# The 32x32 triangular blocks of a gated delta rule: 31 substitution steps on GpSimd in place of 15 steps and a merge on TensorE

## The chip, the cores and the metric

The kernel runs on one core of a Trainium2 chip, in one launch. The metric is the device time of a run in microseconds, and a version's time is the median over its runs. The core has a matrix engine (TensorE, PE in the profile), three engines for elementwise work (VectorE: DVE, ScalarE: ACT, GpSimd: POOL) and 16 DMA engines. DMAs are issued here mostly from the queue of SyncE (SP), some from POOL and ACT. Each engine takes its instructions in order and waits on semaphores for the others.

## The reference

One residual block works on 512 frames of width 1024. A projection feeds two token mixers, a gated delta rule with 8 heads and a convolution branch. Gates merge them, and a SwiGLU channel mixer follows. The change lies in the delta rule, whose chunks hold C frames (64 in the reference):

```python
gc = jnp.cumsum(g, axis=-1)
decay = jnp.exp(jnp.where(tril, gc[..., :, None] - gc[..., None, :], -jnp.inf))
kk = jnp.einsum("bnhid,bnhjd->bnhij", k, k)
m_low = jnp.where(strict, beta[..., :, None] * kk * decay, 0.0)
t_mat = m_low + jnp.eye(CHUNK, dtype=jnp.float32)
rhs = jnp.concatenate([v * beta[..., None], k * (beta * jnp.exp(gc))[..., None]], axis=-1)
sol = lax.linalg.triangular_solve(t_mat, rhs, left_side=True, lower=True, unit_diagonal=True)
...
def step(S, xs_c):
    v_new = u_c - jnp.einsum("bhcd,bhde->bhce", w_c, S)
    o_c = jnp.einsum("bhcd,bhde->bhce", qd_c, S) + jnp.einsum("bhij,bhje->bhie", a_c, v_new)
    S = S * el_c[..., None, None] + jnp.einsum("bhcd,bhce->bhde", kd_c, v_new)
```

So each head needs the inverse of unit triangular matrices, and then a recurrence over chunks that uses them. The output is the whole block's, with a final RMSNorm.

## The kernel before, in words

The kernel takes chunks of 128 frames, four to a head (`NT = 4`), so four 128x128 unit triangular matrices are inverted for each of the 8 heads. The inverse is built from small blocks upward.

The first phase, up to some 475 us, is a row of projections: 32 units for the heads (k, q, v and z of each), 12 for the convolution branch and 16 for the gates. A unit (`proj`) has 8 K steps of three matmuls each (`split3` on L118, a weight in a high and a low part). Its weight is loaded into `raw` by SP (L105), split into `whi` by ACT (L108) and `wlo` by DVE (L109), each in three buffers. The generator `step` walks through the K steps and counts them in `count`. A head owns 32 counts, and behind each head stand 12 or 8 counts of other units (`OTHERS`).

Three pieces of a head hang on this count:

- `front(h)` makes the matrix. It transposes and squares k, multiplies k with itself (L418), scales and masks it into `Un` (L421 on ACT, L422 on POOL) and copies the four diagonal 32x32 blocks into `cp` (L428). Behind the first head, all that `front` puts on POOL is queued behind the last substitution step of the head before (`issue_after(last[0].ins)`).
- The substitution, also in `front`, inverts the diagonal blocks. Coefficients go to DRAM (`sc`, L437) and come back broadcast over the partitions (`U`, L440), both on SP's queue. Then come the steps on POOL, each a multiply into `ytm` (L454) and an add into `y` (L456). Before the change the blocks are 16x16 and the steps 15; the masks `mh1` and `mh2` put the two 16x16 halves of each 32x32 block side by side.
- `chain(h)` takes `y` and is started when the count reaches `START + 32 h` plus the `OTHERS` of the heads before. It first merges pairs of 16x16 blocks to 32x32 (L481 to L498, with matmuls on L490 and L496), then 32 to 64 (L514, L522) and 64 to 128 (L534, L539). Then it runs the recurrence over four chunks (L552 to L578). Each `yield n` lets n counts pass. At its end a power on POOL (L586) gives the norm's factor, which ACT uses in `scaled` (L592) once 32 counts have passed.

Several tiles that the chain reads (`kT`, `qT`, `Un`, `Vp`, `at`, `kd`, `y`) have three buffers, so head h + 3 needs the chain of head h to be done with them.

The order on each engine is set by a planner that puts the instructions in order by their place in the program and by when it holds their inputs to be ready; `behind` and `issue_after` add edges that fix an order on one engine. From count 335 on, weight loads also start work for the later phases (`fill`): DRAM to DRAM copies and accumulating DMAs for sums of FFN weights (`feed_one`, L189 on SP and L193 on POOL), and sums of the down projection's weights (`half_load`, L163, and `dsums_add`, L169, L170, on POOL). The accumulating DMAs and the additions on POOL are queued behind `last[0]`, the last substitution step so far. Before the change the half loads of the first phase take a buffer of `U`.

The phases behind the first one multiply the two mixers' outputs, norm, and run the FFN. They don't touch the substitution.

Of the kernel before, what the change touches and what calls it, by code (L numbers as in the profile page):

```python
# [6 lines left out]
F32 = mybir.dt.float32  # L7
# [16 lines left out]
PAD3 = 368  # L24
START = 84
# [6 lines left out]
def block_kernel(ctx, tc, a):  # L32
# [17 lines left out]
    cst = base.tile([P, 7 * P + 18], F32, name="cst")  # L50
    ident, tri, suf, mid, ones, neg = (cst[:, i * P:(i + 1) * P] for i in range(6))

    mc = cst[:, 6 * P:7 * P]

    mh1, mh2, idc = cst[:, 7 * P:7 * P + 1], cst[:, 7 * P + 1:7 * P + 2], cst[:, 7 * P + 2:]
# [295 lines left out]
    Ye = gp.tile([P, NT, P], F32, name="Ye")  # L351
    for t in (X, Y, Q1, Q2, Xd, Yd, Yl, Ye):
        G.memset(t, 0.0)
# [45 lines left out]
    def front(h, kT, DT):  # L399
# [25 lines left out]
        cc = gp.tile([P, NT, 16], F32, name="cc")  # L425
# [3 lines left out]
        if h:  # L429
            G.tensor_scalar(out=cc, in0=cp[:, :, 0:16], scalar1=mh1, scalar2=None, op0=ALU.mult)  # L430
            G.tensor_scalar(out=cp[:, :, 0:16], in0=cp[:, :, 16:32], scalar1=mh2, scalar2=None, op0=ALU.mult)
            c_ = G.tensor_tensor(out=cc, in0=cc, in1=cp[:, :, 0:16], op=ALU.add)
# [4 lines left out]
        nc.sync.dma_start(sc.rearrange("b k n c -> (b k) n c"), cc)  # L437
        U = gp.tile([P, 16, NT, 16], F32, name="U", bufs=2)
        for b in range(8):
            nc.sync.dma_start(U[16 * b:16 * b + 16].rearrange("p k n c -> p (k n c)"),  # L440
                              sc[b].rearrange("k n c -> (k n c)").partition_broadcast(16))

        Ud = gp.tile([P, NT, P], F32, name="Ud", bufs=3)
        with tc.issue_after(c_.ins) if h else nullcontext():
            G.tensor_tensor(out=Ud, in0=Un, in1=mc.rearrange("p (a t) -> p a t", a=1).broadcast_to([P, NT, P]),
                            op=ALU.mult)


        y = gp.tile([P, NT, 16], F32, name="y", bufs=3)
        S.copy(out=y, in_=idc.rearrange("p (a c) -> p a c", a=1).broadcast_to([P, NT, 16]))  # L450
        for k in range(15):
            w = 15 - k
            tm = gp.tile([P, NT, 16], F32, name="ytm")
            G.tensor_tensor(out=tm[:, :, 0:w], in0=U[:, k, :, k + 1:],  # L454
                            in1=y[:, :, k:k + 1].broadcast_to([P, NT, w]), op=ALU.mult)
            last[0] = G.tensor_tensor(out=y[:, :, k + 1:], in0=y[:, :, k + 1:], in1=tm[:, :, 0:w], op=ALU.add)  # L456
        return ss, kd, b2, Un, Ud, y
# [839 lines left out]
```

## Time and profile before

| | us |
|---|---|
| median of 3 runs | 963.17 |
| lowest and highest of the runs | 961.48 and 963.8 |
| span of the profiled execution, first to last instruction | 961.9 |
| mean granted TensorE clock in it | 0.998 |

The profiled execution has no time of its own beside its span. The span lies within the runs shown, 1.3 us below their median.

A row of the profile names the line of the kernel, the engine and the operation, then the tile that is written and those that are read, the shape, and the count. After the bar it gives the busy time in us and the mean of one instruction in ns, then the idle time of the engine ahead of them and what ended it. A row of the timeline begins with the start and the duration in us; PE's matmuls overlap, so two of them can be busy at once.

### The profile page before, as it was taken

The page shows a single profiled execution, that of the slowest core. Times are in us where ns is not written, and L with a number is a line of the kernel's source. Part 1 is how long each engine was busy: PE and PEld are TensorE (multiplying, and loading weights), DVE is VectorE, ACT ScalarE, POOL GpSimd, SP SyncE. Part 2 cuts the span into 40 slices and gives each one's busy share as a digit, 9 for nine tenths or more (in the row PEclk, how much of TensorE's full clock was granted, in tenths as well). Part 3 has the DMA queues.
Part 4 walks back from the last instruction along what each step waited for, and adds up shares of the span by engine and source line. Part 5 has one row for each costly group of instructions (what it writes and reads, how often), then busy time and mean ns, then how long its engine had stood idle before and what let it go on. Part 6 is the DMA issues. An engine that isn't in the chain of part 4 may idle for free.

```text
span 961.9 us, 14869 instructions
## 1 busy us (share of the span) xinstructions
PE 941.8 (98%) x5199; PEld 793.8 (83%) x5199; DVE 731.8 (76%) x1118; ACT 529.4 (55%) x1095; POOL 357.4 (37%) x565
## 2 busy tenths in 40 slices
PE   6999999999999999999999999999999999999996
PEld 5687888888887887888887888888889999988885
DVE  4898888988888888888477763676525887889886
ACT  6588865867856775544547232423324545556554
POOL 0323645243463327534345342245451111134034
PEclk9999999999999999999999999999999999999999
DMA  9243423133231426988897985499899556578653
GB/s 310 94 143 101 123 66 92 59 116 102 66 103 55 129 82 176 279 253 248 257 297 221 288 277 175 174 272 281 294 252 224 191 184 193 174 221 268 212 192 134
DMA packets 78298, 177.39 MB, mean 184 GB/s; under 512 B 10208, under 2 KB 19328, under 8 KB 77200
## 3 DMA queue, kind: packets, MB, share of 16 engines
q1 hardware_dynamic: 66816, 144.88, 45.4%
q0 software_dynamic: 10256, 28.89, 13.3%
q10 hardware_dynamic: 1152, 2.69, 0.7%
q8 instruction: 41, 0.67, 0.3%
q14 instruction: 33, 0.27, 0.1%
HBM read 156.22 MB, written 45.37 MB: 210 GB/s over the span
## 4 chain that ended last, share of the span: by engine, by line
PE 90%; DVE 4%; ACT 2%; POOL 2%; issue 1%; DMA 1%; SPq 0%; POOLq 0%; ACTq 0%; DVEq 0%
PE mm L118 59%; PE w L118 20%; PE g L385 1%; PE st L564 1%; PE g L418 1%; PE st L558 1%; DVE wlo L109 1%; PE b L490 1%; PE st L563 1%; PE b L496 1%; DMA gsl<-sgd 1%; POOL ss L879 1%; PE b L514 1%; PE st L552 1%; PE g L467 1%
## 5 line engine op out<-in xcount | busy, mean ns | idle before, releaser
L108 ACT ACTIVATE whi<-raw 128x1024 fp32r<-128x1024 f32 (+1 forms) x191 | 196.4, 1030 | 246.8 <-PE mm L118 151.1
L109 DVE TENSOR_TENSOR wlo<-raw,whi 128x1024 fp32r<-128x1024 f32 (+1 forms) x191 | 242.3, 1270 | 95.9 <-ACT whi L108 95.3
L118 PE MATMUL mm<-hh,whi 128*128 128x512 f32 (+1 forms) x688 | 269.9, 393 | 0.5 <-ACT whi L108 0.3
L118 PE MATMUL mm<-hl,whi 128*128 128x512 f32 (+1 forms) x688 | 264.0, 384 | 2.3 <-POOL hl L300 1.6
L118 PE MATMUL mm<-hh,wlo 128*128 128x512 f32 (+1 forms) x688 | 263.9, 384 | 0.1
L620 DVE SCALAR_TENSOR_TENSOR cps<-c,c31w,cps 128x512 f32<-128x512 f32 x240 | 180.2, 751 | 4.3
L118 PEld LDWEIGHTS mm<-hl,whi 128*128 128x128 f32 x688 | 129.9, 189 | 24.7 <-POOL hl L300 2.9
L118 PEld LDWEIGHTS mm<-hh,wlo 128*128 128x128 f32 x688 | 129.6, 188 | 23.8 <-DVE wlo L109 0.6
L118 PEld LDWEIGHTS mm<-hh,whi 128*128 128x128 f32 x688 | 129.8, 189 | 22.7 <-ACT whi L108 0.8
L949 POOL TENSOR_TENSOR fm<-fm 128x256 f32<-128x256 f32 x33 | 29.8, 904 | 113.3 <-DVE s L949 90.1
L372 DVE SCALAR_TENSOR_TENSOR acc<-mm,c4w,acc 128x511 f32<-128x511 f32 (+2 forms) x72 | 53.0, 738 | 1.9 <-ACT acc L369 1.9
L118 PE MATMUL mm<-yh,whi 128*128 128x512 f32 x128 | 50.7, 396 | 0.0
L118 PE MATMUL mm<-yl,whi 128*128 128x512 f32 x128 | 50.0, 391 | 0.6 <-DVE yl L808 0.6
L454 POOL TENSOR_TENSOR ytm<-U,y 128x60 f32<-128x60 f32 (+14 forms) x120 | 31.8, 265 | 48.6 <-DMA U<-sc 30.9
L118 PE MATMUL mm<-yh,wlo 128*128 128x512 f32 x128 | 49.8, 389 | 0.0
L118 PE MATMUL w<-hh,wlo 128*128 128x256 f32 x168 | 47.7, 284 | 0.3 <-DVE wlo L109 0.3
L118 PE MATMUL w<-hh,whi 128*128 128x256 f32 x168 | 47.6, 284 | 0.0
L118 PE MATMUL w<-hl,whi 128*128 128x256 f32 x168 | 47.5, 283 | 0.0
L118 PE MATMUL w<-wlo,fh 128*128 128x512 f32 (+1 forms) x115 | 44.3, 385 | 0.2 <-DVE wlo L109 0.2
L118 PE MATMUL w<-whi,fl 128*128 128x512 f32 (+1 forms) x115 | 44.2, 384 | 0.0
L118 PE MATMUL w<-whi,fh 128*128 128x512 f32 (+1 forms) x115 | 44.2, 384 | 0.0
L456 POOL TENSOR_TENSOR y<-y,ytm 128x60 f32<-128x60 f32 (+14 forms) x120 | 39.0, 325 | 9.4
(324 smaller groups left out, 1904.0 us busy)
## 6 DMA issues: line engine op xcount, KB each, us to landing
raw<-in_win_dram SPq DMA_DIRECT2D x61, 512.0 KB, 3.5
raw<-in_wgu_dram SPq DMA_DIRECT2D x32, 512.0 KB, 3.5
s<-in_wgu_dram SPq DMA_DIRECT2D x48, 256.0 KB, 6.2
raw<-s SPq DMA_DIRECT2D x48, 256.0 KB, 3.8
raw<-wsum SPq DMA_DIRECT2D x44, 256.0 KB, 4.0
raw<-in_wdn_dram SPq DMA_DIRECT2D x33, 256.0 KB, 3.3
s<-in_wgu_dram POOLq DMA_DIRECT2D x24, 256.0 KB, 6.9
s<-s POOLq DMA_DIRECT2D x24, 256.0 KB, 7.0
```

Source lines behind the costliest of these rows:

```text
L108: marked(S.activation(hi, raw, AF.Copy), "unit")
L109: marked(V.tensor_tensor(out=lo, in0=raw, in1=hi.bitcast(F32), op=ALU.subtract), "unit")
L118: marked(PE.matmul(ps, l, r, start=first and i == 0, stop=last and i == 2))
L372: marked(V.scalar_tensor_tensor(out=acc[:, s:], in0=ps[:, :T - s], scalar=c4w[:, j, k:k + 1], in1=acc[:, s:], op0=ALU.mult, op1=ALU.add))
L385: PE.transpose(ps[:, n, :], src[:, n, :], ident)
L418: PE.matmul(ps[:, n, :], kT[:, n, :], kT[:, n, :], start=True, stop=True)
L454: G.tensor_tensor(out=tm[:, :, 0:w], in0=U[:, k, :, k + 1:], in1=y[:, :, k:k + 1].broadcast_to([P, NT, w]), op=ALU.mult)
L456: last[0] = G.tensor_tensor(out=y[:, :, k + 1:], in0=y[:, :, k + 1:], in1=tm[:, :, 0:w], op=ALU.add)
L467: PE.matmul(ps[:, n, :], kT[:, n, :], qT[:, n, :], start=True, stop=True)
L490: PE.matmul(ps[:, n, 0:16], Ud[:, n, :], xc[:, n, 0:16], start=True, stop=True)
L620: V.scalar_tensor_tensor(out=acc, in0=c[:, k:k + T], scalar=c31w[:, i, k:k + 1], in1=acc, op0=ALU.mult, op1=ALU.add)
L949: return eng.tensor_tensor(out=out, in0=in0, in1=in1, op=op)
```

## The change

The substitution works on the four 32x32 diagonal blocks of a matrix in 31 steps, so `y` leaves POOL as the inverse of 32x32 blocks. The merge of 16x16 blocks goes, and with it `Ud`, `Ye`, `Q0`, the masks and the constants for them. The coefficients go to DRAM in eight stores (rows 0 to 15 of each block whole, rows 16 to 31 with their second half only) and come back in four broadcast loads of 32 partitions. `U` grows from 4 KB to 12 KB per partition and has one buffer where it had two. The half loads of the first phase get a tile of their own with one buffer. The chain of head 0 starts 8 counts later and that of head 1 by 4 counts; the others keep their count. The first `yield`s of the chain (2 and 2) go with the merge. The padding is resized.

```diff
-PAD3 = 368
-START = 84
+PAD3 = 482
+START = (92, 88, 84, 84, 84, 84, 84, 84)
...
     def half_load():
         k, cs = halves.pop(0)
-        if len(gps_) == 1:
-            r = gps_[0].tile([P, 16, NT, 16], F32, name="U", bufs=2)
-            r = r.rearrange("p k n c -> p (k n c)").rearrange("p (i c) -> p i c", i=4)
-        else:
-            r = gps_[1].tile([P, 4, 256], F32, name="wsh", bufs=1)
+        r = gps_[-1].tile([P, 4, 256], F32, name="wsh", bufs=1)
...
         for b in range(4):
             b32 = slice(32 * b, 32 * b + 32)
             (G.tensor_copy if h else S.copy)(out=cp[b32], in_=Un[b32, :, b32])
-        if h:
-            G.tensor_scalar(out=cc, in0=cp[:, :, 0:16], scalar1=mh1, scalar2=None, op0=ALU.mult)
-            G.tensor_scalar(out=cp[:, :, 0:16], in0=cp[:, :, 16:32], scalar1=mh2, scalar2=None, op0=ALU.mult)
-            c_ = G.tensor_tensor(out=cc, in0=cc, in1=cp[:, :, 0:16], op=ALU.add)
-        else:
-            S.activation(cc, cp[:, :, 0:16], AF.Copy, scale=mh1)
-            V.scalar_tensor_tensor(out=cc, in0=cp[:, :, 16:32], scalar=mh2, in1=cc, op0=ALU.mult, op1=ALU.add)
-        sc = dram.tile([8, 16, NT, 16], F32, name="sc")
-        nc.sync.dma_start(sc.rearrange("b k n c -> (b k) n c"), cc)
-        U = gp.tile([P, 16, NT, 16], F32, name="U", bufs=2)
-        for b in range(8):
-            nc.sync.dma_start(U[16 * b:16 * b + 16].rearrange("p k n c -> p (k n c)"),
-                              sc[b].rearrange("k n c -> (k n c)").partition_broadcast(16))
-
-        Ud = gp.tile([P, NT, P], F32, name="Ud", bufs=3)
-        with tc.issue_after(c_.ins) if h else nullcontext():
-            G.tensor_tensor(out=Ud, in0=Un, in1=mc.rearrange("p (a t) -> p a t", a=1).broadcast_to([P, NT, P]),
-                            op=ALU.mult)
-        y = gp.tile([P, NT, 16], F32, name="y", bufs=3)
-        S.copy(out=y, in_=idc.rearrange("p (a c) -> p a c", a=1).broadcast_to([P, NT, 16]))
-        for k in range(15):
-            w = 15 - k
-            tm = gp.tile([P, NT, 16], F32, name="ytm")
-            G.tensor_tensor(out=tm[:, :, 0:w], in0=U[:, k, :, k + 1:],
+        sc = dram.tile([4, 3072], F32, name="sc")
+        U = gp.tile([P, 3072], F32, name="U")
+        for b in range(4):
+            nc.sync.dma_start(sc[b, 0:2048].rearrange("(k n c) -> k n c", k=16, n=NT), cp[32 * b:32 * b + 16])
+            nc.sync.dma_start(sc[b, 2048:].rearrange("(k n c) -> k n c", k=16, n=NT),
+                              cp[32 * b + 16:32 * b + 32, :, 16:])
+        for b in range(4):
+            nc.sync.dma_start(U[32 * b:32 * b + 32], sc[b].partition_broadcast(32))
+        U1 = U[:, 0:2048].rearrange("p (k n c) -> p k n c", k=16, n=NT)
+        U2 = U[:, 2048:].rearrange("p (k n c) -> p k n c", k=16, n=NT)
+        y = gp.tile([P, NT, 32], F32, name="y", bufs=3)
+        S.copy(out=y, in_=idc.rearrange("p (a c) -> p a c", a=1).broadcast_to([P, NT, 32]))
+        for k in range(31):
+            w = 31 - k
+            u = U1[:, k, :, k + 1:] if k < 16 else U2[:, k - 16, :, k - 15:]
+            tm = gp.tile([P, NT, 32], F32, name="ytm")
+            G.tensor_tensor(out=tm[:, :, 0:w], in0=u,
                             in1=y[:, :, k:k + 1].broadcast_to([P, NT, w]), op=ALU.mult)
             last[0] = G.tensor_tensor(out=y[:, :, k + 1:], in0=y[:, :, k + 1:], in1=tm[:, :, 0:w], op=ALU.add)
...
-    def chain(h, kT, qT, ss, kd, b2, Un, Ud, Vp, at, yq, zs):
+    def chain(h, kT, qT, ss, kd, b2, Un, Vp, at, y, zs):
         sq = junk[:, 0:P]
-        y = gp.tile([P, NT, 32], F32, name="yb")
         xc = gp.tile([P, NT, 32], F32, name="xc")
-        flat = lambda t: t.rearrange("p n c -> p (n c)")
-        S.activation(y[:, :, 0:16], yq, AF.Copy, scale=mh1)
-        S.activation(y[:, :, 16:32], yq, AF.Copy, scale=mh2)
-        V.transpose(out=flat(xc), in_=flat(y))
-        for b in range(4):
-            b32 = slice(32 * b, 32 * b + 32)
-            S.copy(out=Ye[b32, :, b32], in_=y[b32])
-        yield 2
-        ps = psb.tile([P, 4, P], F32, name="b")
-        for n in range(NT):
-            PE.matmul(ps[:, n, 0:16], Ud[:, n, :], xc[:, n, 0:16], start=True, stop=True)
-        Q0 = gp.tile([P, NT, 16], F32, name="Q0")
-        S.activation(Q0, ps[:, :, 0:16], AF.Copy)
-        yield 2
-        ps = psb.tile([P, 4, P], F32, name="b")
-        for n in range(NT):
-            PE.matmul(ps[:, n, 0:16], Ye[:, n, :], Q0[:, n, :], start=True, stop=True)
-        V.tensor_tensor(out=xc[:, :, 0:16], in0=xc[:, :, 0:16], in1=ps[:, :, 0:16], op=ALU.add)
-        V.transpose(out=flat(y), in_=flat(xc))
+        V.transpose(out=xc.rearrange("p n c -> p (n c)"), in_=y.rearrange("p n c -> p (n c)"))
         yield 1
...
-        if nh < H and count[0] >= START + 32 * nh + sum(OTHERS[:nh]):
+        if nh < H and count[0] >= START[nh] + 32 * nh + sum(OTHERS[:nh]):
```

More of the change, by code (lines that the diff above doesn't have):

```diff
@@ L49, in block_kernel @@
     base.tile([P, PAD3], F32, name="pad")
-    cst = base.tile([P, 7 * P + 18], F32, name="cst")
+    cst = base.tile([P, 6 * P + 32], F32, name="cst")
     ident, tri, suf, mid, ones, neg = (cst[:, i * P:(i + 1) * P] for i in range(6))
-    mc = cst[:, 6 * P:7 * P]
-    mh1, mh2, idc = cst[:, 7 * P:7 * P + 1], cst[:, 7 * P + 1:7 * P + 2], cst[:, 7 * P + 2:]
+    idc = cst[:, 6 * P:]
     vec = small.tile([P, 90], F32, name="vec")
@@ L350, in block_kernel @@
     Yl = gp.tile([P, NT, 64], F32, name="Yl")
-    Ye = gp.tile([P, NT, P], F32, name="Ye")
-    for t in (X, Y, Q1, Q2, Xd, Yd, Yl, Ye):
+    for t in (X, Y, Q1, Q2, Xd, Yd, Yl):
         G.memset(t, 0.0)
@@ L424, in front @@
         cp = gp.tile([P, NT, 32], F32, name="cp")
-        cc = gp.tile([P, NT, 16], F32, name="cc")
         for b in range(4):
@@ L734, in head @@
         with behind(), tc.issue_after(last[0].ins) if h else nullcontext():
-            ss, kd, b2, Un, Ud, y = front(h, k_, DT)
+            ss, kd, b2, Un, y = front(h, k_, DT)
         v_ = yield from v
@@ L743, in second @@
             Vp, at = front2(k_, q_, v_, DT, ss)
-            done.append((h, k_, q_, ss, kd, b2, Un, Ud, Vp, at, y, z_))
+            done.append((h, k_, q_, ss, kd, b2, Un, Vp, at, y, z_))
             yield 0
```

5 lines of the change are left out of this document (2 added, 3 removed).

## The prediction

> **What bounds the kernel now.** I read the page first: the engines' shares, then the slices.
>
> ```profile
> span 961.9 us, 14869 instructions
> PE 941.8 (98%) x5199; PEld 793.8 (83%) x5199; DVE 731.8 (76%) x1118; ACT 529.4 (55%) x1095; POOL 357.4 (37%) x565
> ...
> PE   6999999999999999999999999999999999999996
> ...
> POOL 0323645243463327534345342245451111134034
> ```
>
> TensorE is busy 98% of the span and full in every slice but the two ends; GpSimd (POOL) is at a third. Next the busy time by stretches; the columns are start:end, length, then PE, weight loads, DVE, ACT and POOL, the granted clock, the DMA engines' share and GB/s.
>
> ```profile
> 170.00:210.00 40.00, 40.00 (x239) 32.76 (x238) 35.65 (x70) 31.01 (x83) 17.25 (x42) 1.00 0.28 87
> ...
> 380.00:420.00 40.00, 39.52 (x227) 32.11 (x227) 36.42 (x64) 19.71 (x49) 21.43 (x28) 1.00 0.92 263
> 420.00:475.00 55.00, 55.00 (x262) 45.68 (x261) 35.80 (x53) 22.44 (x43) 21.21 (x25) 1.00 0.85 253
> ```
>
> The eight heads run from about 60 to 380 us. There PE has no gap at all, the clock is full, POOL works 17 of 40 us and the DMA engines are at 0.28. So what leaves PE is gained, unless something else makes PE wait. The question is whether POOL's longer work stays hidden.
>
> **The change part by part.**
>
> *The merge leaves PE.* Two groups of eight matmuls per head go (L490, L496). The timeline of PE in the seventh head:
>
> ```profile
> 363.09 0.96 PE L490 MATMUL b<-xc,Ud 128*128 128x16 f32 x8
> 363.90 0.47 PE L118 MATMUL mm<-hh,whi 128*128 128x512 f32 x1
> 364.22 0.39 PE L118 MATMUL mm<-hl,whi 128*128 128x512 f32 x1
> 364.44 0.40 PE L118 MATMUL mm<-hh,wlo 128*128 128x512 f32 x1
> ...
> 365.37 0.96 PE L496 MATMUL b<-Q,Ye 128*128 128x16 f32 x8
> 366.18 0.48 PE L118 MATMUL mm<-hh,whi 128*128 128x512 f32 x1
> 366.50 0.40 PE L118 MATMUL mm<-hl,whi 128*128 128x512 f32 x1
> ```
>
> Matmuls overlap, so the price is read from start to start. Each group holds PE for 0.81 us (363.09 to 363.90, 365.37 to 366.18). The projection matmul behind it takes 0.32 us to the next start instead of the usual 0.23 (364.22 to 364.44), another 0.09. That is 0.9 us per group, 1.8 per head, 14.4 for eight heads. Where the group stands beside other small matmuls these pay the 0.09 anyway, so the lower end is 13.0. I take 14, or 1.75 per head. The copies on ACT, the additions and one transpose on DVE, and the two half-masked copies that went with the merge, are off the path already: PE had no gap for them. They are costed at nothing, and their going can only help.
>
> *The substitution doubles its steps and widens them.* One head's 15 step pairs, POOL's timeline without a disturbance:
>
> ```profile
> 152.96 0.29 POOL L454 TENSOR_TENSOR ytm<-U,y 128x60 f32<-128x60 f32 x1 [5.75 <-DMA U<-sc]
> ...
> 153.72 0.29 POOL L454 TENSOR_TENSOR ytm<-U,y 128x56 f32<-128x56 f32 x1
> ...
> 161.64 0.21 POOL L454 TENSOR_TENSOR ytm<-U,y 128x8 f32<-128x8 f32 x1
> ...
> 162.21 0.21 POOL L454 TENSOR_TENSOR ytm<-U,y 128x4 f32<-128x4 f32 x1
> ...
> 162.50 0.21 POOL L456 TENSOR_TENSOR y<-y,ytm 128x4 f32<-128x4 f32 x1
> ```
>
> A pair (multiply and add) takes 0.76 us at 60 elements and 0.57 to 0.58 at 8: about 0.58 plus 0.0036 per element above 12. That gives 15 x 0.58 + 0.0036 x 312 = 9.8 us for the 15 pairs, and the rows give 9.75 (152.96 to 162.71). For 31 pairs of 124 down to 4 elements the same line gives 31 x 0.58 + 0.0036 x 1624 = 23.8 us. Not every step is undisturbed:
>
> ```profile
> L454 POOL TENSOR_TENSOR ytm<-U,y 128x60 f32<-128x60 f32 (+14 forms) x120 | 31.8, 265 | 48.6 <-DMA U<-sc 30.9
> ...
> L456 POOL TENSOR_TENSOR y<-y,ytm 128x60 f32<-128x60 f32 (+14 forms) x120 | 39.0, 325 | 9.4
> ```
> ```profile
> 120.22 1.27 POOL L456 TENSOR_TENSOR y<-y,ytm 128x48 f32<-128x48 f32 x1
> ```
> ```profile
> 120.13 1.23 DVE L109 TENSOR_TENSOR wlo<-raw,whi 128x1024 fp32r<-128x1024 f32 x1
> ```
>
> A step that meets the DVE subtraction of a weight split (L109) lasts 1 us longer. All 240 steps are busy 70.8 us, 8.85 per head; the undisturbed head is busy about 7.5 (9.75 less 30 gaps of 0.075). So disturbance adds 1.35 us to each 9.75, or 14%, and 23.8 becomes 27 us. Bounds are 24 (none met) and 28.5 (the first head's stretch has more splits). POOL's serial work grows by some 16 us per head.
>
> *POOL's other work and the loop.* The next head's work on POOL is issued behind the last step, so POOL runs a loop: power, Un, the copies, wait for U, 31 pairs.
>
> ```profile
> L422 POOL TENSOR_TENSOR Un<-Un,DT 128x512 f32<-128x512 f32 x8 | 11.1, 1383 | 15.7 <-ACT Un L421 15.7
> L428 POOL COPY cp<-Un 32x128 f32<-32x128 f32 x28 | 9.8, 350 | 1.3
> ...
> L412 POOL TENSOR_TENSOR ss<-ss,root 128x4 f32<-128x4 f32 x8 | 8.1, 1015 | 83.4 <-DVE ss L410 83.4
> ```
>
> 1.0 + 1.4 + 4 x 0.35 = 3.8 us. The waits behind these rows vanish when POOL comes late. Ud and the three cc operations go.
>
> *The way through DRAM.* Nine DMAs per head on SP become twelve: one store and eight loads become eight small stores and four loads of 393 KB (32 partitions x 12 KB).
>
> ```profile
> 146.00 0.33 SPq L437 DMA_DIRECT2D sc<-cc  x1
> 147.46 3.56 SPq L440 DMA_DIRECT2D U<-sc  x8
> ```
> ```profile
> raw<-in_win_dram SPq DMA_DIRECT2D x61, 512.0 KB, 3.5
> U<-sc SPq DMA_DIRECT2D x64, 64.0 KB, 2.3
> ```
> ```profile
> SPq L105 <- DVE wlo L109: 387.1, 116, 17.1
> SPq L437 <- POOL cc L432: 38.4, 7, 9.5
> ```
>
> Eight stores at 0.33 are 2.6 us, 1.0 of it beside the copies that are still running: 1.6 after the last copy. Then a load's issue of 0.4, its fixed part of about 2.1, and 1.57 MB of data. Between 64 KB (2.3 us) and 512 KB (3.5) the rows give 373 KB/us, so 4.2 us, and 5.6 beside the 28% of other traffic. Sum 9.7, lower bound 8.3. The upper bound goes by the rate at which the small loads are sent, 64 KB per 0.46 us: 11.3 us of data, sum 15.4. I take 9.3, near the lower end, since the big loads are nearest in size to the 512 KB row. Behind a store that waits on SP stand weight loads (raw). SP already stood up to 9.5 us there, and otherwise SP waits 387 us for free raw buffers, so the loads run ahead; I cost this at nothing up to some 12 us.
>
> [...] No transfer of this size to 32 partitions is in this trace; the eight to 16 partitions show no queueing.
>
> The loop is then 27 + 3.8 + 9.3 = 40 us per head, from 24 + 3.8 + 8.3 = 36 to 28.5 + 3.8 + 15.4 = 48.
>
> *When y is due.* First the rows of the first and the last of eight heads:
>
> ```profile
> 78.67 1.20 ACT L428 COPY cp<-Un 32x128 f32<-32x128 f32 x4
> ```
> ```profile
> 83.80 4.21 SPq L440 DMA_DIRECT2D U<-sc  x8
> ```
> ```profile
> 112.44 0.30 DVE L498 STREAM_TRANSPOSE yb<-xc 128x128 f32<-128x128 f32 x1
> ```
> ```profile
> 113.72 0.25 PE L514 MATMUL b<-Xd,Un 128*32 128x32 f32 x2
> ...
> 405.59 0.25 PE L514 MATMUL b<-Xd,Un 128*32 128x32 f32 x2
> ```
> ```profile
> 374.52 1.84 POOL L193 DMA_DIRECT2D s<-in_wgu_dram  x2
> ```
>
> The first matmul that needs y is now L514, and the transpose and four copies ahead of it take 1.3 to 1.4 us (112.44 to 113.72). A count of the schedule is one K step, three matmuls, 0.68 us. L514 stood 2+2+1 counts behind the chain's start and now stands 1. With START 92, 88, 84 in place of 84 it falls 4 counts later for head 0, at the same count for head 1, and 4 earlier for the rest. Less 1.75 us per merge gone, y is due at 113.72 + 2.7 - 1.75 - 1.4 = 113 for head 0, and at 405.59 - 2.7 - 14 - 1.4 = 387.5 for head 7.
>
> Head 0's y: copies on ACT end at 79.9, stores and loads put U at about 89 (before, its loads went out from 83.80 to 88), and 28 us of steps make 117. Head 7's: 117 + 7 x 40 = 397. So head 0 is 4 us late and head 7 9.5 us in all. The matmul is late with y; PE then waits unless projections can go ahead of it. Head 7 has the 16 gate units behind it, which need no y, so I count half of its last 5: PE waits 6 to 7 us. A delay once paid moves every later due time, so waits do not add up beyond the largest lateness.
>
> *POOL's later work.* The DMA accumulations and weight sums begin behind the last step: 374.52 before, some 20 us later now. POOL is then busy 21 of 40 and 21 of 55 us, so it catches up; the DMA engines, at 0.92 and 0.85, are the cover that is thin. I take 0 and keep 2 us as the upper end. The single buffer for the half loads can hold SP for a store, which the raw lead covers.
>
> **Sum.** 961.9 - 14 + 6.5 = 954.4 in the profile's terms. The runs' median is 963.17, 1.3 above the profiled span (all three lie in 961.48 to 963.8), so 955 us.
>
> **The rivals.**
>
> 1. *The whole merge time is gained.* If the loop is at most 38 us and head 0's y comes by 114, nothing waits: 963.2 - 14 = 949, down to 947 with the 14.4 and earlier chains. For it: 24 us of steps without disturbance and 8.3 for U make 36. Against: DVE splits fall into every stretch.
>
> 2. *POOL's loop sets the pace: slower.* Place: POOL between one head's last step and the next. At 42 us per head, y of head 7 comes at 117 + 294 = 411, 23.5 us late; PE waits that long where its order holds the chain's matmuls ahead of projections: 963.2 - 14 + 23.5 = 973. It decides from 14 us of lateness, a loop of 40.6. For it: U's loads, the one price far from its rows, need only 2 us more. Against: the gates can fill for heads 6 and 7, which would leave about 965. [...]
>
> 3. *The gain is used up.* A loop of 40.4 to 40.9 leaves 960 to 966, no measurable change. That the merge's PE time is not freed speaks against the stretch rows, where PE has no gap.
>
> **How the numbers follow.** A run of this kernel tells 0.3%, about 2.9 us, from no change. Forecast (950 to 960): 0.47. Rival 1: 0.13. Rival 3: 0.14. Rival 2 (966 to 980): 0.26. Faster: 0.47 + 0.13 = 0.60; same 0.14; slower 0.26. The range leaves out a tenth at the upper end: 947 to 972. The forecast's own range is 950 to 960.
>
> **What would show it.** L490 and L496 gone and PE busy near 928 us. L454 and L456 x248 each, pairs near 1 us at 124 elements, 26 to 28 us per head, POOL busy some 470 us. U's loads landing within 7 us of their issue. L514 of head 0 near 117, with PE idle ahead of it for DVE's transposed copies. First accumulation DMA on POOL near 395. The prediction is wrong if POOL's loop is over 41 us, if DVE standing at the transpose holds back splits (PE waiting for wlo), if ACT's scaling stands behind the power (L586) that is now queued behind longer steps, or if PE starves for raw.

## The result and the profile after

The changed kernel takes 1036.29 us (median of 4 runs, 1033.31 to 1037.3) against 963.48 us beside it: ratio 1.0753, 95% interval 1.0735 to 1.0772. It is 73 us slower; the forecast was 955 us, the range 947 to 972. The profiled execution has a span of 1033.6 us. Line numbers below are those of the changed kernel where its rows are shown.

The page, with the rows that answer to those of before:

```profile
span 1033.6 us, 14793 instructions
PE 948.7 (92%) x5071; PEld 797.1 (77%) x5071; DVE 731.3 (71%) x1101; ACT 514.8 (50%) x1038; POOL 438.2 (42%) x791
PE   7999797978879798979769999999999999999996
PEclk9999898989899898989989999999999999999999
```

128 matmuls have gone, yet PE is busy 7 us longer. Its row has sixes, sevens and eights up to the 21st slice (about 540 us) and is full from there on; the clock row dips in most of the same slices. So the loss lies in the first phase. The stretches say it in one number (columns: start:end, length, busy time with the count in brackets for PE, weight loads, DVE, ACT, POOL, then granted clock, DMA share, GB/s). First before, then after:

```profile
90.00:450.00 360.00, 359.02 (x2066) 292.99 (x2065) 315.86 (x586) 233.95 (x636) 168.74 (x367) 1.00 0.42 127
450.00:570.00 120.00, 119.39 (x524) 97.36 (x523) 76.29 (x88) 54.56 (x76) 49.52 (x52) 1.00 0.88 272
```
```profile
90.00:450.00 360.00, 310.62 (x1676) 253.18 (x1675) 270.69 (x498) 197.50 (x529) 221.08 (x557) 0.92 0.38 107
450.00:570.00 120.00, 105.08 (x483) 84.10 (x483) 70.12 (x103) 43.61 (x84) 44.76 (x55) 0.93 0.81 247
```

PE starts 390 matmuls fewer in the same 360 us, 128 of them the merge's own, and 41 fewer in the next 120. Matching every weight matmul (L118 before, L115 after) of the two traces by its number, the later start is some 51 us where the changed kernel stands at 450 us, 70 us at 560 us and 72 us from 600 us on.

The chain that ended last was 90% PE before. Now more than a third of it is POOL and DMA:

```profile
PE 49%; POOL 22%; DMA 14%; issue 5%; ACT 3%; SPq 3%; DVE 3%; POOLq 0%; ACTq 0%; DVEq 0%
```

POOL's loop, from head 0's last step to head 1's first, by the timelines of POOL and of SP's queue:

```profile
93.43 0.40 POOL L439 TENSOR_TENSOR ytm<-U,y 128x124 f32<-128x124 f32 x1 [11.72 <-DMA U<-sc]
...
120.13 0.21 POOL L441 TENSOR_TENSOR y<-y,ytm 128x4 f32<-128x4 f32 x1
120.28 1.01 POOL L404 TENSOR_TENSOR ss<-ss,root 128x4 f32<-128x4 f32 x1
121.28 1.28 POOL L414 TENSOR_TENSOR Un<-Un,DT 128x512 f32<-128x512 f32 x1
122.62 2.20 POOL L419 COPY cp<-Un 32x128 f32<-32x128 f32 x4
...
137.89 0.40 POOL L439 TENSOR_TENSOR ytm<-U,y 128x124 f32<-128x124 f32 x1 [10.89 <-DMA U<-sc]
...
441.89 0.21 POOL L441 TENSOR_TENSOR y<-y,ytm 128x4 f32<-128x4 f32 x1
```
```profile
123.00 0.73 SPq L424 DMA_DIRECT2D sc<-cp  x1
...
127.47 0.56 SPq L425 DMA_DIRECT2D sc<-cp  x1
128.12 1.92 SPq L428 DMA_DIRECT2D U<-sc  x4
```
```profile
DMA to landing us min/median/max: 4.2/6.1/8.1
```

Steps 26.9 us (93.43 to 120.3), front 4.5 (120.28 to 124.82), and 13.1 from the last copy to the first step. In these 13.1 us the eight stores go out 0.64 us apart, to 128.0; the four loads follow, 0.5 us apart, and land 4.2 to 8.1 us after their issue, one every 1.8 us. From first step to first step it is 44.5 us here. Over seven loops (first steps at 93.43 and 414.19) it is 45.8 us: on average 27.7 of steps, 4.4 of front and 13.7 from the last copy to the first step. Head 0's y is done at 120.3, head 7's at 442.1.

Who waits (engine and line, what it waited for: us in all, times, longest):

```profile
POOL ytm L439 <- DMA U<-sc: 102.2, 8, 13.8
ACT Vp L449 <- POOL ss L404: 40.8, 6, 8.4
DVE xc L464 <- POOL y L441: 34.5, 6, 6.6
```
```profile
SPq L160 <- DMA wsum<-wsh: 90.0, 12, 12.2
```

ACT stands for the pow, DVE for y, and SP until a half-load's buffer has been stored (L160; before, L163 stood 40.7 us for this, 8.5 of them for the buffers of U).

### The profile page after: what moved, and what is told of

It is laid out like the page before. It is cut to its first block, busy times and chain, and to the rows that moved or that the text cites. A ratio compares the mean times of both kernels' runs of the same rounds, so it can differ in the third digit from the quotient of the medians.

```text
span 1033.6 us, 14793 instructions
## 1 busy us (share of the span) xinstructions
PE 948.7 (92%) x5071; PEld 797.1 (77%) x5071; DVE 731.3 (71%) x1101; ACT 514.8 (50%) x1038; POOL 438.2 (42%) x791
## 4 chain that ended last, share of the span: by engine, by line
PE 49%; POOL 22%; DMA 14%; issue 5%; ACT 3%; SPq 3%; DVE 3%; POOLq 0%; ACTq 0%; DVEq 0%
PE mm L115 28%; PE w L115 19%; POOL ytm L439 8%; POOL y L441 7%; DMA U<-sc 5%; DMA wsum<-wsh 3%; DMA wsh<-in_wdn_dram 3%; DMA s<-in_wgu_dram 2%; POOL wsh L166 2%; POOL sacc L616 1%; DMA DT<-mrow 1%; SPq L425 1%; SPq L428 1%; SPq L424 1%; DVE wlo L106 1%
## 5 line engine op out<-in xcount | busy, mean ns | idle before, releaser
L106 DVE TENSOR_TENSOR wlo<-raw,whi 128x1024 fp32r<-128x1024 f32 (+1 forms) x191 | 242.1, 1269 | 102.3 <-ACT whi L105 101.5
L115 PE MATMUL mm<-hh,whi 128*128 128x512 f32 (+1 forms) x688 | 273.6, 398 | 3.4 <-ACT whi L105 2.2
L115 PE MATMUL mm<-hl,whi 128*128 128x512 f32 (+1 forms) x688 | 268.5, 390 | 2.3 <-POOL hl L293 1.6
L115 PE MATMUL mm<-hh,wlo 128*128 128x512 f32 (+1 forms) x688 | 267.8, 390 | 0.7 <-DVE wlo L106 0.7
L586 DVE SCALAR_TENSOR_TENSOR cps<-c,c31w,cps 128x512 f32<-128x512 f32 x240 | 180.4, 752 | 4.9 <-ACT cps L584 0.3
L115 PEld LDWEIGHTS mm<-hh,whi 128*128 128x128 f32 x688 | 133.4, 194 | 27.7 <-ACT whi L105 2.8
L115 PEld LDWEIGHTS mm<-hl,whi 128*128 128x128 f32 x688 | 133.1, 194 | 26.0 <-POOL hl L293 2.9
L115 PEld LDWEIGHTS mm<-hh,wlo 128*128 128x128 f32 x688 | 132.8, 193 | 25.5 <-DVE wlo L106 1.6
L439 POOL TENSOR_TENSOR ytm<-U,y 128x124 f32<-128x124 f32 (+30 forms) x248 | 90.7, 366 | 121.0 <-DMA U<-sc 102.2
L441 POOL TENSOR_TENSOR y<-y,ytm 128x124 f32<-128x124 f32 (+30 forms) x248 | 88.5, 357 | 19.3
L166 POOL TENSOR_TENSOR wsh<-wsh 128x256 f32<-128x256 f32 x56 | 47.0, 839 | 75.9 <-DMA wsh<-in_wdn_dram 72.8
L115 PE MATMUL mm<-yl,whi 128*128 128x512 f32 x128 | 50.1, 392 | 1.8 <-DVE yl L774 1.8
L115 PE MATMUL mm<-yh,whi 128*128 128x512 f32 x128 | 50.8, 397 | 0.2 <-ACT yh L773 0.2
L115 PE MATMUL mm<-yh,wlo 128*128 128x512 f32 x128 | 49.9, 390 | 0.0
L115 PE MATMUL w<-hh,wlo 128*128 128x256 f32 x168 | 47.8, 284 | 0.3 <-DVE wlo L106 0.3
L115 PE MATMUL w<-hh,whi 128*128 128x256 f32 x168 | 47.7, 284 | 0.0
L115 PE MATMUL w<-hl,whi 128*128 128x256 f32 x168 | 47.5, 283 | 0.0
L115 PE MATMUL w<-wlo,fh 128*128 128x512 f32 (+1 forms) x115 | 44.3, 385 | 0.2 <-DVE wlo L106 0.2
L115 PE MATMUL w<-whi,fl 128*128 128x512 f32 (+1 forms) x115 | 44.2, 385 | 0.0
```

The costliest lines, as they stand in the source:

```text
L106: marked(V.tensor_tensor(out=lo, in0=raw, in1=hi.bitcast(F32), op=ALU.subtract), "unit")
L115: marked(PE.matmul(ps, l, r, start=first and i == 0, stop=last and i == 2))
L166: G.tensor_tensor(out=o, in0=x, in1=y, op=ALU.add)
L439: G.tensor_tensor(out=tm[:, :, 0:w], in0=u, in1=y[:, :, k:k + 1].broadcast_to([P, NT, w]), op=ALU.mult)
L586: V.scalar_tensor_tensor(out=acc, in0=c[:, k:k + T], scalar=c31w[:, i, k:k + 1], in1=acc, op0=ALU.mult, op1=ALU.add)
```

## The experiments

Each edit moves the planner's order on all engines a little, so a difference is that of the edit and its order; `e11` below shows that an order alone can cost 12 us.

**The gain by itself (`e1`).** The kernel before without the two matmul groups, the copy to `Q0` and the addition (the inverse lacks that block):

```diff
-            PE.matmul(ps[:, n, 0:16], Ud[:, n, :], xc[:, n, 0:16], start=True, stop=True)
-            PE.matmul(ps[:, n, 0:16], Ye[:, n, :], Q0[:, n, :], start=True, stop=True)
-        V.tensor_tensor(out=xc[:, :, 0:16], in0=xc[:, :, 0:16], in1=ps[:, :, 0:16], op=ALU.add)
```

> The kernel before, without the merge's 8 + 8 matmuls per head, the copy of Q0 and the addition (the inverse of the 32x32 blocks is left incomplete; the 16x16 steps, the transposes, the copies and the counts stay). Theory (the merge's time on TensorE was a real cost, 1.75 us per head): 963.5 - 14 = 949.5 us, between 948.5 and 951. Rival (the freed time turns into another wait, so the gain never was there): 960 to 963.5 us.

948.21 us, ratio 0.9844 (0.9828 to 0.986), 0.3 us under the theory's range. The merge's 15 us are there to be had. What the new substitution costs is therefore not 73 but 88 us. This run and the changed kernel start the same 5071 matmuls, so the page splits the 88:

```profile
PE 925.5 (98%) x5071; PEld 779.0 (82%) x5071; DVE 725.4 (77%) x1110; ACT 527.3 (56%) x1087; POOL 364.0 (38%) x565
```

Of the 87.5 us between the two spans (946.1 and 1033.6), PE stands for 64 us more and is busy for 23 us longer (948.7 against 925.5) with the same work, at a mean granted clock of 0.963 against 0.998.

**The steps (`e2`).** The changed kernel with `for k in range(15)` in place of 31; steps 16 to 31 are left out.

> The changed kernel with only the first 15 of the 31 substitution steps on GpSimd (the other 16 are left out, so the blocks stay incomplete); stores, loads, order and counts as changed. Theory (GpSimd's loop of 46 us per head sets the pace): the loop falls by some 12 us to 34, below TensorE's 39 to 40 per head, TensorE's stalls at the heads go, and the sums of FFN weights begin some 85 us earlier: 950 to 975 us, what is left being the single buffer of the half loads. Rival (the loads of U, the DMA traffic or the clock cost the time whatever the number of steps): above 1010 us.

974.7 us, 1.0122 (1.01 to 1.0145), just inside the theory's range: 62 of the 88 us come back. The loop is 38.3 us (first steps at 93.1 and 361.1 us), and the last y is done at 376 us, before the 387.5 at which it is due.

**The half-loads (`e3`).** Two buffers (`wsh`, bufs 1 to 2, room taken from a pad).

> The changed kernel with two buffers for the half loads in the first phase instead of one (the padding made smaller for it). Theory (two losses: GpSimd's loop costs some 50 us up to 450 us, and the single buffer costs some 20 us behind it, where SP stands in front of the gates' stores): 1036 - 15 to 20 = 1016 to 1021 us. Rival (the late start of GpSimd's weight sums alone makes the second loss): 1030 to 1036 us.

1017.23 us, 1.0554 (1.0535 to 1.0572): 19 us back, as expected, and in the expected place:

```profile
450.00:570.00 120.00, 117.59 (x551) 94.89 (x552) 88.25 (x116) 52.92 (x96) 63.96 (x66) 0.98 0.89 268
```

PE is busy 117.6 of 120 us there, against 105.1 with one buffer.

**U's loads over two queues (`e4`).**

```diff
-            nc.sync.dma_start(U[32 * b:32 * b + 32], sc[b].partition_broadcast(32))
+            (nc.sync if b < 2 else nc.gpsimd).dma_start(U[32 * b:32 * b + 32], sc[b].partition_broadcast(32))
```

> The changed kernel with U's loads for partitions 64 to 127 issued from GpSimd's queue, beside those for 0 to 63 on SP's. [...]

1050.79 us, 1.0902 (1.0877 to 1.0927), 14.5 us slower than the changed kernel: a miss, since the author's estimate was 1006 to 1016 us, with the loads landing sooner. They don't; with one queue the median was 6.7 us:

```profile
U<-sc SPq DMA_DIRECT2D x16, 384.0 KB, 7.1
U<-sc POOLq DMA_DIRECT2D x16, 384.0 KB, 7.3
```

Half of the loads now stand in GpSimd's order too, so this run says nothing on what limits them.

**The next head's front inside the steps.** Three kernels: steps 1 to 16, then pow, product and copies of the next head, then steps 17 to 31 (`e5`); U in two tiles besides (`e6`); two half-load buffers besides (`e7`). The cores of the edits:

```diff
+        if h:
+            tail[0](cpi)                  # steps 17 to 31 of the head before, behind this head's copies
...
-        U = gp.tile([P, 3072], F32, name="U")
+        U1 = gp.tile([P, 2048], F32, name="U1")
+        U2 = gp.tile([P, 1024], F32, name="U2")
```

> The changed kernel, with the order on GpSimd written anew: steps 1 to 16 of a head, then the next head's pow, product and four copies, then steps 17 to 31. Theory (the POOL loop of 45.8 us sets the pace up to 450 us, and of it 3.8 us are the next head's front, 13 us the way through DRAM, 27 to 28 us the steps): the eight stores now run beside steps 17 to 31, but U has one buffer, so its four loads still come behind step 31: loop 28 + 4 + 9 = about 40 us, last y near 405 us where the changed kernel has 442 us, time 990 to 1012 us (1000). Rival 1 (the wait of ACT for the next head's pow, 40.8 us, is the loss and not the loop): that wait is gone here too, so this run alone does not part them; 995. Rival 2 (the way through DRAM is held up by other transfers on the queue, not by its place in the loop): loop unchanged at 45 us, 1030 us.

> As the run with the front inside the steps, and U as two tiles, one of the 16 first rows and one of the 15 last, loaded by eight broadcasts, so the next head's first rows can land beside steps 17 to 31. Theory: the loop is 28 + 4 = 32 us plus what of 13 us of stores and loads steps 17 to 31 (about 12 us) do not cover, but no shorter than TensorE brings the next head (about 36 us): 34 to 37 us; last y near 375 us, before it is due (387.5 us), no PE stall over 3 us on the substitution before 450 us; what is left over the kernel without the merge (948 us) is the wait for the half-load buffer behind GpSimd's weight sums, 19 us at most: 955 to 978 us (967). Rival (time is lost to GpSimd's and VectorE's sharing, or to the clock of TensorE, and not to the loop): over 985 us with the loop under 38 us.

> As the run with two tiles of U, and two buffers for the half-loads that GpSimd sums (which alone took 19 us off the changed kernel). Theory: both losses are gone and the merge's 14 to 15 us stay won: 945 to 958 us (950), faster than the kernel before (963 us). Rival (GpSimd's sums, moved back by the steps, are themselves late and not just short of a buffer): 958 to 975 us, with GpSimd busy until past 560 us and TensorE waiting for weights.

1041.83 us, 1.0805 (1.0772 to 1.0838); 1046.89, 1.087 (1.0847 to 1.0892); 1031.4, 1.0703 (1.0681 to 1.0725). All miss, and on the slow side, `e7` beyond its rival's range too. The loop got shorter in none (46 to 48 us), which was the sign of `e5`'s second rival, but the waits show another reason than other transfers on the queue. In `e7` U is no longer waited for, but the next head is:

```profile
POOL ss L404 <- DVE ss L402: 91.6, 6, 29.7
POOL ytm L445 <- DMA U<-sc: 10.5, 4, 9.1
```

POOL keeps its order, so y now waits in the middle of its steps for the next head's k, which PE, itself stalled for 66 us between 85 and 600 us, brings late. (A stall is here and below the time between the starts of two matmuls, where it is over 0.6 us, less the usual 0.23.) A wait of 92 us took the place of one of 102.

**The pow alone (`e8`).** It goes among the steps of the head before, near step 7.

> The changed kernel, with the next head's pow alone put among the steps of the head before (near step 7); its product and copies stay behind step 31. ACT's scaled copies of V wait 40.8 us in all for that pow. Theory (the loop sets the pace, and the wait for the pow lies beside the same lateness): the loop stays at 45 us, so TensorE then waits for y instead: 1020 to 1036 us (1030). Rival (the pow's wait holds ACT, and behind it TensorE's projections, by itself): 990 to 1005 us, with the loop still at 45 us.

1044.39 us, 1.0843 (1.0808 to 1.0877); the theory's range ended at 1036. ACT's wait for the pow is gone from the trace, and VectorE's for y has grown from 34.5 us:

```profile
DVE xc L475 <- POOL y L450: 59.4, 7, 13.2
```

Taking away ACT's wait alone gains nothing while y is late.

**More time for each head in PE's order.** `OTHERS` to eight times 16 (`e9`), and eight times 20 (`e10`), both with two half-load buffers; and 16 in the kernel before (`e11`).

> The changed kernel with two buffers for the half-loads (alone: 1017 us), and 16 units of other projection work between two heads on TensorE's order instead of 12 (heads 0 to 3) and 8 (heads 4 to 7). A head's 32 units and its 12 or 8 take about 41 or 38 us by the spacing of the heads before the change (480 units in some 450 us, 0.94 us each); GpSimd's loop takes 45.8 us, so y falls behind its place in the order by 4 to 8 us more with every head. With 16 units a head has 48 x 0.94 = 45 us. Theory (y comes late against the order that was laid out for a shorter loop, and the engines work in order, so VectorE and TensorE stand): the loop stays at 45 us, the stalls of TensorE between 85 and 600 us fall from some 50 us to under 20 us, 950 to 975 us (962). Rival (what the runs with the front moved inside showed, 1031 to 1047 us, is GpSimd's and VectorE's sharing, or the clock, and not the order): 1005 to 1020 us with the stalls unchanged.

> As the run with 16 units, with 20: 52 units, 49 us for a head. Theory: y is there before its place in the order is reached; stalls under 12 us, but the last head's recurrence then begins at unit 448 of 480 and its end has no projections beside it (some 10 us): 950 to 975 us (960). Rival (sharing or clock): 1005 to 1020 us.

> The kernel before, with 16 units of other work a head instead of 12 and 8, to see what that alone is worth. Theory: nothing is late in the kernel before, so there is nothing to give back: 960 to 967 us. Rival (the order with 16 is better for its own sake): under 955 us.

1010.43 us, 1.0487 (1.0466 to 1.0508); 1046.8, 1.0864 (1.0837 to 1.089); 975.09, 1.012 (1.0104 to 1.0137). Two misses, and the control fell outside both of its cases: 16 costs the kernel before 12 us. If that cost simply adds, `e9` gains 7 + 12 = 19 us on the 1017 us. That agrees with lateness only in sign. By its time `e9` lies in the rival's range, and the sum of PE's stalls is unchanged (50 us, as in `e3`); they have only moved, from before 450 us to behind it. With 20 POOL's loop grew to some 54 us (first steps at 93.74 and 472.6 us), paced by late heads. The part of the rivals that blames GpSimd's and VectorE's sharing (in the prediction's rows a step that meets a weight split lasts 1 us longer) finds nothing in VectorE's own times: in the changed kernel a `wlo` takes 1269 ns on average where it took 1270, and a convolution step 752 where it took 751. GpSimd's steps are near the length that was foreseen (27.7 us a head, against 27).

**The way through DRAM taken out (`e13`).** U is loaded for head 0 alone; heads 1 to 7 use its coefficients.

```diff
-        for b in range(4):
-            nc.sync.dma_start(U[32 * b:32 * b + 32], sc[b].partition_broadcast(32))
+        if not h:
+            U0.append(U)
+            for b in range(4):
+                nc.sync.dma_start(U[32 * b:32 * b + 32], sc[b].partition_broadcast(32))
```

> The changed kernel, with U loaded for head 0 alone and used again by the other seven heads (the stores stay); the sums in these heads are so made with head 0's coefficients. GpSimd's order stays: pow, product, copies, steps. Theory (y(7) is 54 us late because the loop is 45.8 us against 39 us a head on TensorE, and 13 of the 45.8 are the way through DRAM): the loop is bound by steps and front at 32 us, or TensorE's 39; stalls of TensorE before 450 us fall from 50 to under 15 us, and the weight sums still wait for their buffer: 980 to 998 us (988). [...]

1023.9 us, 1.0623 (1.0605 to 1.064): a miss, only 12 us back. The loop did not become short: it is still 43.6 us, and the last y is done at 425 us. POOL now stands for the next head's k in place of U, and the waits name another piece of the heads that stands in POOL's order behind steps:

```profile
POOL ss L404 <- DVE ss L402: 69.8, 5, 21.2
ACT DT L388 <- POOL DT L385: 42.1, 4, 15.0
```

**The same, with that addition on VectorE (`e18`)** (`G.tensor_tensor` to `V.tensor_tensor` on L385).

> As the run with U loaded once for all heads (1024 us, where ACT waited 42 us for GpSimd's additions of DT, which the order had put behind steps), with the addition of DT on VectorE, so that the way through DRAM is out of the loop without that wait; half-loads in one buffer as in the changed kernel. Heads 1 to 7 use head 0's coefficients. Theory: 968 to 992 us (980): the 50 us of the heads gone, the buffer's 19 us left. Rival (the way through DRAM is not what the heads wait for): 1010 to 1030 us.

978.79 us, 1.0175 (1.0149 to 1.0201), as the theory said (980): 57 us less than the changed kernel. The last y:

```profile
381.55 0.21 POOL L444 TENSOR_TENSOR y<-y,ytm 128x4 f32<-128x4 f32 x1
```

It is done at 381.8 instead of 442.1, ahead of the 387.5 at which it is due; the loop is 37.1 us. The run differs from the changed kernel in two things, U's loads and DT's place, and none was made with DT's addition moved alone.

**Forms that compute all of it, with the front off GpSimd.** The product `Un` on VectorE, the copies on ACT, two half-load buffers (`e14`); U in two tiles besides (`e15`); and both with DT's addition on VectorE (`e17` and `e16`).

```diff
-        G.tensor_tensor(out=Un, in0=Un, in1=DT, op=ALU.mult)
+        V.tensor_tensor(out=Un, in0=Un, in1=DT, op=ALU.mult)
-            (G.tensor_copy if h else S.copy)(out=cp[b32], in_=Un[b32, :, b32])
+            S.copy(out=cp[b32], in_=Un[b32, :, b32])
```

> The changed kernel, with the product Un = Un x DT on VectorE and the four copies on ACT for all heads, so that of the front only the pow is left on GpSimd, and two buffers for the half-loads. The stores can then run beside the steps of the head before, and nothing of the next head stands among the steps (what spoiled the runs with the front moved inside: GpSimd waited 92 us for the next head there). Theory: loop 28 + 9.3 (four loads behind step 31) + 0.3 = 38 us, TensorE's own 39 us bounds it; y(7) near 395 us, 6 to 8 us late as y(0): 950 to 968 us (957). Rival (the loop does not matter, see the run with U loaded once): 1000 to 1017 us.

> As the run with the front off GpSimd, and U as two tiles, loaded by eight broadcasts, so that the next head's first 16 rows can land beside steps 17 to 31. Theory: loop bounded by TensorE (39 us) with GpSimd waiting for the next head's loads; only the first y is late; the merge's 15 us stay won: 945 to 962 us (951). Rival (what is lost is lost by GpSimd's steps beside VectorE): 1000 to 1017 us.

> As the run with the front off GpSimd and U in two tiles (1020 us, with stalls of 22 us at 104 us and ACT waiting 29 us for GpSimd's additions of DT, which stood behind 31 steps), and the addition of DT on VectorE too: of the heads only the steps and the two pows are left on GpSimd. Theory (every piece of the heads that stands behind a run of 62 step instructions in GpSimd's order, y, pow, DT, holds ACT, VectorE and then TensorE; with the steps alone on it and a loop under 39 us nothing is held): 948 to 968 us (958), stalls before 450 us under 15 us. [...]

> As the run with the front off GpSimd and two buffers (989 us), and the addition of DT on VectorE: U has one buffer, the loop stays at 38 to 42 us with the four loads in it, so y and pow stay some us late. Theory: 965 to 990 us (977), between that run and the one with U in two tiles. Rival: no change, 985 to 993 us.

989.16 us, 1.026 (1.0238 to 1.0282); 1020.02, 1.0589 (1.0571 to 1.0607); 987.66, 1.0261 (1.0242 to 1.0279); 995.57, 1.0344 (1.0326 to 1.0363). `e14` and `e16` give 28 and 30 us back beyond the buffers' 19, and all four are slower than the theory's ranges, by 6 to 58 us. In `e14` and `e16` the loop is still 41.7 us, and the last y comes at 412 and 411 us, some 24 late. Moving DT's addition gains 32 us with U in two tiles and loses 6 with one. In `e16` one stall is left that is longer than 4 us. PE, SP's queue, VectorE and ACT there:

```profile
128.78 0.80 PE L115 MATMUL mm<-hh,whi 128*128 128x512 f32 x1 [24.59 <-ACT whi L105]
```
```profile
105.89 11.59 SPq L430 DMA_DIRECT2D U<-sc  x8
117.58 1.32 SPq L102 DMA_DIRECT2D raw<-in_win_dram  x3
```
```profile
103.39 22.91 DVE L587 SCALAR_TENSOR_TENSOR cps<-c,c31w,cps 128x512 f32<-128x512 f32 x29
```
```profile
126.34 0.60 ACT L589 ACTIVATE cv<-cps 128x512 f32<-128x512 f32 x1 [8.15 <-DVE cps L587]
```

SP stands at head 1's loads until head 0's steps free U, and three weights stand behind them. VectorE's order has 29 convolution steps in that gap, and ACT's `cv`, which stands ahead of the next `whi`, waits for them. That wait ended last, at 126.3 us, some 9 us after SP was free.

**Those loads behind the weights (`e19`).** Head 1's stores and loads are put behind the three weight loads on SP's queue (`issue_after(loads[-1].ins)`), and the pow may go early.

> As the run with U in two tiles and the addition of DT off GpSimd (987.7 us), which had one long stall, 24.9 us at 104 us: SyncE's queue held head 1's eight loads of U from 105.9 to 117.5 us, until head 0's steps had freed U, and three weight loads stood behind them. Here head 1's stores and loads of U are put behind those three weight loads on SyncE's queue, and the next head's pow may go ahead of the steps. Theory (that stall is the queue's): it falls to under 8 us, the rest stays: 960 to 974 us (966). Rival (the stall is that of VectorE, which had 29 steps of the 31-tap convolution in a row there, and ACT behind them): it stays over 15 us, 980 to 992 us.

993.06 us, 1.0315 (1.0297 to 1.0334). The stall at 104 us is gone. That does not show that it was the queue's: the planner has also put 5 convolution steps there in place of 29, so the theory and its rival changed together. The time is not gone: SP now stands from 112.4 to 124.1 us, and weights stand behind it again.

```profile
112.43 11.68 SPq L439 DMA_DIRECT2D U<-sc  x8
124.21 2.32 SPq L102 DMA_DIRECT2D raw<-in_win_dram  x3
```

The stalls of PE between 85 and 600 us sum to 36.5 us here and to 37.4 in `e16`. No form that computes all of it beats the kernel before.

## Why the prediction was wrong

Three steps failed: the price of the way through DRAM, the main reason that POOL's loop is 45.8 us a head and not 40; the claim that a late y costs PE only its own lateness; and the half loads' single buffer, which was taken at nothing and costs 19 us. The part-by-part account follows.

*The merge leaves PE: right.* 14 us foreseen, 15 measured (`e1`).

*The steps: right.* 27 us a head foreseen with collisions; 26.9 measured for head 0, 27.7 on average.

```profile
L439 POOL TENSOR_TENSOR ytm<-U,y 128x124 f32<-128x124 f32 (+30 forms) x248 | 90.7, 366 | 121.0 <-DMA U<-sc 102.2
L441 POOL TENSOR_TENSOR y<-y,ytm 128x124 f32<-128x124 f32 (+30 forms) x248 | 88.5, 357 | 19.3
```

POOL is busy 179.2 us with them in all, or 22.4 a head, and 62 gaps of 0.075 make 27.

*The way through DRAM: the first step that failed.* 9.3 us foreseen; 13.1 measured after the last copy in the first loop, 13.7 on average. The stores were priced at 0.33 us from the row of one store; eight in a row go out every 0.64, so 3.2 us follow the copies' end where 1.6 stood. The loads were priced at 5.6 us for four and take 1.8 each, 7.2: 384 KB every 1.8 us is some 213 KB/us, where the rows of 64 and 512 KB had given 373. The prediction's other price, 11.3 us at the rate at which the small loads were sent, was too high. What sets the rate of these loads, no run here shows.

*The front: 3.8 us foreseen, 4.4 measured.* In the first loop the copies take 2.2 us, not 1.4; later they take 1.3, but from the third loop on the norm's power (L552) stands ahead of the next head's pow, for 1.0 us.

*The loop: 40 us foreseen, 45.8 measured.* With TensorE's own (387.5 - 113) / 7 = 39 us a head the difference is not 1 us but 6.6 us a head. y(0) was foreseen at 117 and came at 120.3; y(7) at 397 and came at 442.1, 54.6 us late and not 9.5. Rival 2 had this mechanism, its place and its point of decision (40.6 us). Its 42 us a loop, an estimate that no run shows, was too small. The prediction saw that "U's loads, the one price far from its rows, need only 2 us more" and still gave it 0.26, since the gates could fill for the last heads; loads and stores needed 3.8 us more, 4.4 on average.

*What lateness costs: counted too narrowly.* The prediction let PE wait for the matmul that needs y, as long as y is late. In the changed kernel a late y stops more than that. PE's timeline at head 2:

```profile
206.56 0.40 PE L115 MATMUL mm<-hh,wlo 128*128 128x512 f32 x1
214.63 0.80 PE L518 MATMUL st<-S,kT 128*128 128x128 f32 x2 [7.68 <-DVE o L543]
...
216.51 0.63 PE L115 MATMUL mm<-hh,wlo 128*128 128x512 f32 x1
216.94 0.63 PE L524 MATMUL st<-R,Y 128*128 128x128 f32 x2
217.49 1.06 PE L480 MATMUL b<-Xd,Un 128*32 128x32 f32 x16
```

The matmul that needs the new y is L480, at 217.49. PE has stopped over 10 us sooner, at 207.0, and stands for 7.7 us at head 1's recurrence (L518), for VectorE's `o` (L543). VectorE and ACT at that time:

```profile
210.91 0.31 DVE L464 STREAM_TRANSPOSE xc<-y 128x128 f32<-128x128 f32 x1 [5.10 <-POOL y L441]
...
214.29 0.29 DVE L543 TENSOR_TENSOR o<-st,R 128x128 f32<-128x128 f32 x1 [2.36 <-ACT R L542]
```
```profile
212.85 1.14 ACT L449 ACTIVATE Vp<-g,ss 128x128 f32<-128x128 f32 x4 [8.45 <-POOL ss L404]
213.87 0.39 ACT L542 ACTIVATE R<-st,sm 128x128 f32<-128x128 f32 x1
```

VectorE stands at head 2's `xc` for y, and ACT at head 3's `Vp` for the pow that POOL does behind head 2's last step. Head 1's recurrence, which needs neither, is queued behind both; here the pow came last (212.85 us, against 210.91 for y). Of the waits that the profile names for PE it is the longest in sum:

```profile
PE st L518 <- DVE o L543: 26.0, 4, 7.7
```

The sum of all PE stalls over 0.6 us between 85 and 600 us is 70 us against 2.3 before.

*The pow that ACT's scaling needs*: the prediction feared it for L586, the norm's. The one that held ACT was the other, L404, for the next head's `Vp`, 40.8 us. `e8` takes it away and gains nothing: VectorE stands for y all the same, and longer.

*POOL's later work: 0 foreseen, 2 at most; 19 measured* (`e3`). "The single buffer for the half loads can hold SP for a store, which the raw lead covers" is the sentence that failed. POOL's first accumulating DMA came at 443.0 us where 374.5 stood and 395 was foreseen. While SP stands for the one buffer (L160, 90.0 us in all), the gates' stores (L600) stand behind it; ACT waits for such a store to land, and PE for ACT:

```profile
ACT sg L599 <- DMA sgd<-sg: 35.3, 7, 10.4
PE b L377 <- ACT o L558: 13.3, 2, 8.0
```

The list of waits of the kernel before has no row of the first kind. With two buffers the stalls between 450 and 600 us fall from 19 to 3 us.

*The sum as the runs tell it:* 948 without the merge; 19 us for the half-load buffer (`e3`); the remaining 69 us, by subtraction, belong to the heads. By the prediction's own rule the lateness of the last y would be 54.6 of them. Two runs that bring the loop under TensorE's 39 us get most of the time back, `e2` with 15 steps (62 us) and `e18` with U loaded once and DT's addition off POOL (57 us). The stalls before 450 us fall in them from 51 us to 18 and 25, and 15 and 13 us of their gain lie behind 450 us, where the buffer's cost was. But both change more than the loop: in `e2` the pow and DT also stand behind fewer steps, and `e13` and `e18` differ in DT's addition alone, and by 45 us. So the runs show that what comes late behind POOL's steps (y, the pow, DT) makes most of the loss; how much is y's alone they do not show. What stands behind 62 step instructions in POOL's order can count as much as the steps' own result.

*What stays open:* in the best six variants (`e2`, `e14`, `e16` to `e19`) 26 to 47 us remain above 948 us, also where y is in time (`e2`, `e18`). The runs show single causes for parts of them (weights behind U's loads on SP, 29 convolution steps in a row on VectorE), but taking one away moved the loss, and the planner's order is new in each. Whether an order exists in which 31 steps on GpSimd beat the merge was not found out.

## What to carry to other kernels

A long serial run on an engine that was two thirds idle (POOL, 37% busy before) was not free here: price its loop against the pace of the engine it feeds (45.8 us a head against 39), with every store and load at the rate of a row of its own kind, and where two prices for a transfer differ (5.6 and 11.3 us for U's loads, 7.2 measured), work the sum through with both. Pieces that shared that engine's queue, and transfers on a queue that waited for it, became late with it (the pow, 40.8 us of ACT's time; the gates' stores, 35.3), so list who waits for each of them. A late input stopped not only its reader but also what stood behind its reader in that engine's order: PE stood 26.0 us for `o`, which needs neither the late y nor the pow.

## What the runs showed of the hardware that was not expected

In the changed kernel TensorE's granted clock was 0.50 behind the stall of 7.7 us above. Windows around that stall (columns as before):

```profile
200.00:206.50 6.50, 6.50 (x43) 5.82 (x42) 5.11 (x8) 4.17 (x7) 5.40 (x15) 1.00 0.71 220
206.50:214.50 8.00, 0.46 (x2) 0.02 (x1) 1.18 (x5) 1.64 (x7) 6.78 (x20) 0.74 0.04 18
214.50:220.50 6.00, 5.87 (x30) 4.91 (x31) 3.13 (x8) 4.87 (x20) 0.82 (x3) 0.50 0.15 29
220.50:226.00 5.50, 5.50 (x31) 4.34 (x29) 4.52 (x13) 2.68 (x6) 0.00 (x0) 1.00 1.02 226
```

The granted clock is 0.50 for 6 us after 8 us of standing, and matmuls that start every 0.23 us at full clock (206.33 to 206.56) start every 0.43 (216.51 to 216.94). Behind the stall of 8.0 us that ends at 539.73 us it is 0.58 from 539.7 to 545.7 us. Half the clock for 6 us is worth up to 3 us, on top of the stall, and it was in no term of the prediction; the 23 us by which PE is busy longer than in `e1` are, as an estimate, the sum of it. What brings the clock down and back, no run here shows.
